# Token spans inside the weight loop: a new order for the products of the fill and the merge of an encoder layer

## The chip, the cores and the metric

The kernel runs on one core of a Trainium2 chip. The metric is the time of one execution on the device in microseconds (us). Lower is better.

## What is computed

The reference is one bidirectional encoder layer with two branches, run over two token groups (1024 prompt tokens and 256 sample tokens, 1280 in all, model width 1024). Cut to what matters here:

```python
h = rmsnorm(x, norm_mix) * (1 + sc1) + sh1
p = h @ w_in                                   # p_mla, p_rwkv, p_gate (2 x 1024 columns)
o_mla  = mla_branch(p_mla, ...) @ w_mla_o      # attention, 8 heads
o_rwkv = rwkv_branch(p_rwkv, ...) @ w_rwkv_o   # a scan over the tokens, both ways
gm, gr = split(sigmoid(p_gate), 2)
x = x + g1 * ((gm * o_mla + gr * o_rwkv) @ w_out)
h = rmsnorm(x, norm_ffn) * (1 + sc2) + sh2
u, z = split(h @ w_ffn_in, 2)
x = x + g2 * ((silu(u) * z) @ w_ffn_out)
return rmsnorm(x, final_norm)
```

All of it is in float32. A matrix product is made of three matmuls on rounded halves (`hi` and `lo`): weights hi by tokens hi, weights hi by tokens lo, weights lo by tokens hi.

## The kernel before

Tokens lie along the free dimension, so that a tile of 128 output rows by n tokens is one accumulation in a bank of PSUM (128 x 512 float32). The stages follow one another: a first norm and the products of `w_in`, attention, then the scan of the rwkv branch, the merge of both branches, and the feed-forward layer with the final norm.

The scan (`phase_rwkv`) works in ten batches of 128 tokens, one after the other through a state `S`. Each batch is a long chain of small matmuls on TensorE, copies on ScalarE and VectorE, and an inversion of 16-wide blocks on VectorE. While it runs, `phase_fill` gives TensorE other work. That is 27 gate products (nine slices `j` of `w_in`, for token spans at 0 and 256, then 512 and 768, then 1024, each 256 wide), then two rounds of eight products with `w_mla_o`: one for tokens 0 to 511, and one for tokens 512 to 1023 together with 1024 to 1279. When it ends, `merge` does eight products with `w_rwkv_o` and eight with `w_out`, first for one span of 512 tokens (`early`, from 256), then for two spans (`late`: 512 tokens from 768, and 256 from 0).

The order of instructions on each engine is not written by hand. A planner works on the emitted program: each instruction has a priority, that of its place in the program or higher (scan steps are emitted with `high_priority`), and by the planner's own costs it puts the one of highest priority that could start into its engine's queue. Each engine then runs its queue in that order. The fill stands behind the scan in priority.

All products that the change touches go through `product` (line 1044). `weights` (line 1040) brings the weights of a product in blocks of 4 x 128 rows: SP loads `wraw`, ScalarE rounds it into `whi` (line 53), and GpSimd subtracts to get `wlo` (line 55). There are two buffers of each (`RB`, `WB` = 2). A product with `kt` = 8 (gates, `w_out`) has two such halves, and so holds both buffers; one with `kt` = 4 (`w_mla_o`, `w_rwkv_o`) has one. `parts` is a list of PSUM tiles, and each part a list of spans of tokens that share the tile side by side. The gates have one part of two spans of 256 (one span in the last nine), the late rounds have two parts of 512 and 256. The generator yields a part as soon as its matmuls are emitted, and the caller then emits what reads it: `gate` a tanh on ScalarE (line 1153), `mla_out` and `merge` a VectorE operation (lines 1189, 1115, 1128).

In `phase_fill` the PSUM pool `g.fp` has two buffers (`FP` = 2); in `merge` it is `g.mm`, with six. Two tile pairs hold the tokens of the gates, tags `x0` and `x1`; `load` (line 1141) fills each with four DMAs (line 1145) when the products that read it are done:

```python
for i, x in enumerate(xs):
    for j in js[len(both):]:
        gate(j, x)
    if s < 2 and i < len(spans[s + 1]):
        new.append(load(i, spans[s + 1][i]))
```

The second round of `mla_out` reads the slots of `x0` and `x1` again, and `mid`, the operand of the early merge, is allocated in the slot of `x1` after it. A row pool of four buffers (`FR` = 4) holds the `gt` and `xm` rows of `merge`: two spans take all four.

Of the kernel before, what the change touches and what calls it, by code (L numbers as in the profile page):

```python
# [6 lines left out]
F32 = mybir.dt.float32  # L7
# [7 lines left out]
P = 128  # L15
# [31 lines left out]
def split_w(g, src, kt, eng=None, tag="w", pool=None, width=P, rbufs=2, bufs=2):  # L47
    nc = g.nc
    pool = pool or g.wst
    raw = pool.tile([P, kt, width], F32, tag=tag + "raw", name="wraw", bufs=rbufs)  # L50
    nc.sync.dma_start(out=raw if len(src.shape) == 3 else raw.rearrange("p (d f) n -> p d f n", d=src.shape[1]), in_=src)
    hi = pool.tile([P, kt, width], F32R, tag=tag + "hi", name="whi", bufs=bufs)
    nc.scalar.copy(hi, raw)  # L53
    lo = pool.tile([P, kt, width], F32R, tag=tag + "lo", name="wlo", bufs=bufs)
    (eng or nc.gpsimd).tensor_tensor(lo, raw, hi, ALU.subtract)  # L55
    return hi, lo
# [983 lines left out]
def weights(g, src, kt):  # L1040
    return [split_w(g, src[:, k0:k0 + 4, :], 4, pool=g.fl, tag=g.ft, rbufs=RB, bufs=WB) for k0 in range(0, kt, 4)]


def product(g, src, kt, parts, ws=None):

    ws = ws or weights(g, src, kt)
    for part in parts:
        p = g.fp.tile([P, 512], F32, tag="mm", name="fp")
        c = 0
        for a, n in part:  # L1050
            for k in range(kt):
                wh, wl = ws[k // 4]
                for i, (ww, aa) in enumerate(((wh, a[0]), (wh, a[1]), (wl, a[0]))):
                    g.nc.tensor.matmul(p[:, c:c + n], lhsT=ww[:, k % 4, :], rhs=aa[:, k, :n],  # L1054
                                       start=(k == 0 and i == 0), stop=(k == kt - 1 and i == 2))
            c += n
        yield p[:, :c]


# [44 lines left out]
def merge(g, spans, ops, m, x1, row):  # L1104

    nc, io = g.nc, g.io
    cs = [slice(c0, c0 + n) for c0, n in spans]
    for dt in range(KT):
        ts = []
        for c, (c0, n) in zip(cs, spans):  # L1110
            ts.append((row("gt")[:, :n], row("xm")[:, :n]))
            for t, nm, k in zip(ts[-1], ("gate", "xm"), (8, 0)):
                nc.sync.dma_start(out=t, in_=g.scr[nm][k + dt, :, c])
        for p, c, (t, xm) in zip(product(g, io["w_rwkv_o"][dt], 4, [[x] for x in ops]), cs, ts):
            nc.vector.scalar_tensor_tensor(t, t, 1.0, p, ALU.add, ALU.mult)
            nc.gpsimd.tensor_tensor(t, t, xm, ALU.add)
            split_in(g, t, m[0][:, dt, c], m[1][:, dt, c])
    for dt in range(KT):
        xs = [row("xt")[:, :n] for _, n in spans]
        for c, x in zip(cs, xs):  # L1120
            nc.sync.dma_start(out=x, in_=io["xT"][dt, :, c])
        for p, x, (c0, n) in zip(product(g, io["w_out"][dt], KT, [[([y[:, :, c] for y in m], n)] for c, (_, n) in zip(cs, spans)]),
                                 xs, spans):
            for s, (s0, l) in enumerate(SEG):
                lo, hi = max(c0, s0), min(c0 + n, s0 + l)
                if lo < hi:
                    r = slice(lo - c0, hi - c0)
                    nc.vector.scalar_tensor_tensor(x1[:, dt, lo:hi], p[:, r], g.gh[:, dt, s:s + 1], x[:, r], ALU.mult, ALU.add)


def phase_fill(g):
# [17 lines left out]
    def gate(j, *parts, ws=None):  # L1149
        for p in product(g, io["w_in"][20 + j], KT, [[x[:2] for x in parts]], ws):  # L1150
            n, c0 = p.shape[-1], parts[0][2]
            t = row("gt", n)
            nc.scalar.activation(t, p, AF.Tanh, scale=0.5)
            nc.sync.dma_start(out=g.scr["gate"][j, :, c0:c0 + n], in_=t)
# [317 lines left out]
```

## Time and profile before

| | |
|---|---|
| median of 3 runs | 2723.12 us (2720.77 to 2726.25) |
| profiled execution | 2719.07 us |
| its span in the trace | 2717.4 us |
| mean granted TensorE clock | 0.957 |
| TensorE busy | 2547.4 us, 94% of the span |
| VectorE, ScalarE, GpSimd busy | 1326.4, 1020.0, 841.7 us |
| chain that ended last: matmuls of line 1054 (`product`) | 8% of the span |

The profile is of one execution; times in it are counted from the span's start. The fill begins at about 880 us and ends at about 1530 us, the merge ends at about 1742 us. A busy TensorE is not one at its peak, since matmuls are pipelined and their ends are modelled: the starts of successive matmuls tell the rate. 1.00 of the granted clock is 2.4 GHz, 0.50 is 1.2 GHz.

### The profile page before, as it was taken

Reading aid. Unit: us, or ns where it says so; the run is one execution under the profiler, and the core shown is the slowest. Engines: PE = TensorE matmul, PEld = TensorE weight load, DVE = VectorE, ACT = ScalarE, POOL = GpSimd, SP = SyncE. Lnnn points to the kernel's source line nnn. Section 1 sums busy time; section 2 is a strip of 40 time slices with the busy share of each in tenths; the row PEclk is TensorE's granted clock in tenths of the full one; section 3 lists DMA queues with packets and bytes.
Section 4 is the critical chain, followed back from the end, with each engine's and each line's share of the span. In section 5 each row is a group of like instructions: output and inputs, shape, how many; then the busy total and the mean of one; then the engine's idle time right before and its main releaser. Section 6 shows DMA issues by size and latency. Waiting matters only on the chain.

```text
span 2717.4 us, 47321 instructions
## 1 busy us (share of the span) xinstructions
PE 2547.4 (94%) x19578; PEld 2160.1 (79%) x19578; DVE 1326.4 (49%) x2138; ACT 1020.0 (38%) x1913; POOL 841.7 (31%) x824
## 2 busy tenths in 40 slices
PE   5999999989997899999998988999999999999997
PEld 3777778778886788988877767778888888888886
DVE  6665562367776374565646557462222222222228
ACT  4433333257676565565653233241110111101114
POOL 1112131011115455454634466342111111111123
PEclk8999999999998798998988989999999999999998
DMA  7655531110013334444445655221111110111113
GB/s 294 226 185 198 188 146 63 45 29 18 20 32 107 103 107 137 141 114 137 126 147 164 191 182 154 92 71 55 39 39 39 39 36 35 39 39 39 39 40 132
DMA packets 178120, 273.80 MB, mean 101 GB/s; under 512 B 15008, under 2 KB 104944, under 8 KB 177904
## 3 DMA queue, kind: packets, MB, share of 16 engines
q1 hardware_dynamic: 164512, 223.19, 25.8%
q0 software_dynamic: 5760, 26.22, 2.4%
q10 hardware_dynamic: 7632, 21.37, 2.3%
q8 instruction: 154, 2.52, 0.4%
q14 instruction: 62, 0.51, 0.1%
HBM read 202.52 MB, written 68.20 MB: 100 GB/s over the span
## 4 chain that ended last, share of the span: by engine, by line
PE 75%; DVE 11%; ACT 5%; DMA 4%; issue 3%; POOL 2%; SPq 0%; DVEq 0%; POOLq 0%; ACTq 0%
PE mm L67 42%; PE fp L1054 8%; PE s L626 3%; PE o L660 2%; PE gps L453 2%; PE pA L819 2%; PE proj L559 2%; PE t L647 2%; PE py L927 2%; DMA ld<-scr_s 1%; PE pS L939 1%; PE py L945 1%; PE lora L369 1%; PE ada_ps L170 1%; PE py L933 1%
## 5 line engine op out<-in xcount | busy, mean ns | idle before, releaser
L55 POOL TENSOR_TENSOR wlo<-wraw,whi 128x512 fp32r<-128x512 f32 (+3 forms) x233 | 406.5, 1748 | 1177.6 <-ACT whi L53 1166.7
L53 ACT CAST whi<-wraw 128x512 fp32r<-128x512 f32 (+2 forms) x248 | 194.5, 789 | 898.0 <-issue 466.7
L67 PE MATMUL mm<-h2h,whi 128*128 128x512 f32 (+1 forms) x1056 | 279.2, 358 | 2.9 <-ACT whi L53 2.9
L67 PE MATMUL mm<-h2h,wlo 128*128 128x512 f32 (+1 forms) x1056 | 278.4, 357 | 1.1 <-POOL wlo L55 1.1
L67 PE MATMUL mm<-h2l,whi 128*128 128x512 f32 (+1 forms) x1056 | 278.2, 357 | 0.0
L67 PE MATMUL mm<-g,whi 128*128 128x512 f32 (+1 forms) x1056 | 240.6, 359 | 6.2 <-DVE ft L1259 5.6
L1054 PE MATMUL fp<-x,whi 128*128 128x256 f32 (+1 forms) x912 | 211.1, 324 | 11.7 <-ACT x L1036 5.0
L67 PEld LDWEIGHTS mm<-g,whi 128*128 128x128 f32 x1056 | 177.8, 190 | 38.0 <-issue 5.7
L67 PEld LDWEIGHTS mm<-h2h,whi 128*128 128x128 f32 x1056 | 177.1, 189 | 34.6 <-ACT whi L53 3.4
L67 PEld LDWEIGHTS mm<-h2h,wlo 128*128 128x128 f32 x1056 | 176.8, 188 | 32.7 <-POOL wlo L55 2.0
L67 PEld LDWEIGHTS mm<-h2l,whi 128*128 128x128 f32 x1056 | 176.9, 188 | 31.2 <-issue 0.5
L1271 DVE SCALAR_TENSOR_TENSOR x<-mm,g2h,x 128x512 f32<-128x512 f32 (+1 forms) x144 | 87.0, 655 | 196.3 <-PE mm L67 196.0
L1054 PEld LDWEIGHTS fp<-x,whi 128*128 128x128 f32 x912 | 157.6, 206 | 23.9 <-ACT x L1036 6.1
L67 PE MATMUL mm<-hl,whi 128*128 128x512 f32 (+1 forms) x480 | 147.5, 364 | 7.7 <-DVE hl L265 7.7
L67 PE MATMUL mm<-hh,whi 128*128 128x512 f32 (+1 forms) x480 | 148.1, 366 | 6.4 <-ACT pp L320 3.8
L1054 PE MATMUL fp<-x,wlo 128*128 128x256 f32 (+1 forms) x456 | 147.8, 325 | 6.3 <-POOL wlo L55 6.3
L1259 DVE SCALAR_TENSOR_TENSOR ft<-ft,mm 128x512 f32<-128x512 f32 (+1 forms) x66 | 36.0, 594 | 225.6 <-ACT ft L1258 225.6
L67 PE MATMUL mm<-hh,wlo 128*128 128x512 f32 (+1 forms) x480 | 145.8, 363 | 0.0
L1260 DVE TENSOR_TENSOR ft<-ft,mm 128x512 f32<-128x512 f32 (+1 forms) x66 | 36.0, 593 | 217.5 <-PE mm L67 217.5
L67 PE MATMUL mm<-g,wlo 128*128 128x512 f32 (+1 forms) x528 | 136.2, 359 | 1.4 <-POOL wlo L55 1.4
L626 PE MATMUL s<-kb,q 128*128 128x512 f32 (+1 forms) x432 | 112.0, 392 | 2.3 <-ACT pr L632 2.2
L67 PEld LDWEIGHTS mm<-hh,whi 128*128 128x128 f32 x480 | 84.5, 191 | 27.8 <-issue 6.9
(331 smaller groups left out, 5239.2 us busy)
## 6 DMA issues: line engine op xcount, KB each, us to landing
wraw<-in_w_ffn_in_dram SPq DMA_DIRECT2D x56, 512.0 KB, 3.5
wraw<-in_w_in_dram SPq DMA_DIRECT2D x68, 256.0 KB, 3.6
araw<-in_w_ada_dram ACTq DMA_DIRECT2D x32, 512.0 KB, 3.6
wraw<-in_w_ffn_out_dram SPq DMA_DIRECT2D x26, 512.0 KB, 3.6
wraw<-in_w_in_dram SPq DMA_DIRECT2D x20, 512.0 KB, 3.8
x<-scr_h SPq DMA_DIRECT2D x20, 512.0 KB, 7.5
araw<-in_w_ada_dram SPq DMA_DIRECT2D x16, 512.0 KB, 9.3
gt<-scr_gate SPq DMA_DIRECT2D x32, 256.0 KB, 2.7
```

What stands on the lines that cost most here:

```text
L53: nc.scalar.copy(hi, raw)
L55: (eng or nc.gpsimd).tensor_tensor(lo, raw, hi, ALU.subtract)
L67: nc.tensor.matmul(p[:, :n], lhsT=ww[:, k, :], rhs=aa[:, k, c0:c0 + n], start=(k == 0 and i == 0), stop=(k == kt - 1 and i == 2))
L453: nc.tensor.matmul(p[:, :n], lhsT=ww[:, k % 4, :], rhs=aa[:, k, c0:c0 + n], start=(k == 0 and i == 0), stop=(k == KT - 1 and i == 2))
L559: nc.tensor.matmul(p[:, :n], lhsT=ww[:, k, :], rhs=aa[:, k, c0:c0 + n], start=(k == 0 and i == 0), stop=(k == kt - 1 and i == 2))
L626: nc.tensor.matmul(s[:, o:o + w], lhsT=a[:, tt * P:(tt + 1) * P], rhs=b[:, c0 + o:c0 + o + w], start=(m == 0), stop=(m == 2))
L647: nc.tensor.transpose(t[:, j, :], prs[i][:, kk * P:(kk + 1) * P], g.ident)
L660: nc.tensor.matmul(o, lhsT=vs[h // 4][:, c0 // P + kk, h % 4, :], rhs=pts[j][m][kk // 4][:, kk % 4, :], start=(kk == 0 and m == 0), stop=( ...
L819: nc.tensor.matmul(pA[e][:, pt], lhsT=bk[HV[e], 2 * pt + sl], rhs=lt[HV[e], pt, e], start=True, stop=True)
L927: nc.tensor.matmul(py[e][HV[r], c, :], lhsT=lt[:, HV[r]], rhs=xv[:, u, e, :], start=(u == 0), stop=(r == 0 and u == 7))
L1054: g.nc.tensor.matmul(p[:, c:c + n], lhsT=ww[:, k % 4, :], rhs=aa[:, k, :n], start=(k == 0 and i == 0), stop=(k == kt - 1 and i == 2))
L1271: nc.vector.scalar_tensor_tensor(x1[:, dt, c0:c0 + n], p[:, :n], g.g2h[:, dt, c0 // TP:c0 // TP + 1], x1[:, dt, c0:c0 + n], ALU.mult, ALU.add)
```

## The change

`product` now emits its matmuls with the spans in the innermost loop. For each block of 128 rows of weights, and for each of the three combinations of halves, all spans of all parts come one after another. All PSUM tiles of the product are taken at its beginning, and all parts are yielded at its end. In a tile that two spans share, only the first span's first matmul has `start`, and only the last span's last has `stop`. Products with a single span come out in the same order as before: those are the last nine gates, the first round of `mla_out`, and the early merge.

```diff
     ws = ws or weights(g, src, kt)
-    for part in parts:
-        p = g.fp.tile([P, 512], F32, tag="mm", name="fp")
+    ps = [g.fp.tile([P, 512], F32, tag="mm", name="fp") for _ in parts]
+    todo, ends = [], []
+    for p, part in zip(ps, parts):
         c = 0
-        for a, n in part:
-            for k in range(kt):
-                wh, wl = ws[k // 4]
-                for i, (ww, aa) in enumerate(((wh, a[0]), (wh, a[1]), (wl, a[0]))):
-                    g.nc.tensor.matmul(p[:, c:c + n], lhsT=ww[:, k % 4, :], rhs=aa[:, k, :n],
-                                       start=(k == 0 and i == 0), stop=(k == kt - 1 and i == 2))
+        for j, (a, n) in enumerate(part):
+            todo.append((p[:, c:c + n], a, n, j == 0, j == len(part) - 1))
             c += n
+        ends.append(c)
+    for k in range(kt):
+        wh, wl = ws[k // 4]
+        for i, (ww, e) in enumerate(((wh, 0), (wh, 1), (wl, 0))):
+            for p, a, n, first, last in todo:
+                g.nc.tensor.matmul(p, lhsT=ww[:, k % 4, :], rhs=a[e][:, k, :n], start=(k == 0 and i == 0 and first),
+                                   stop=(k == kt - 1 and i == 2 and last))
+    for p, c in zip(ps, ends):
         yield p[:, :c]
```

## Rows read from the trace of the kernel before

**Rows 1.** Busy time of the engines in stretches of the scan and fill, in us, with the number of instructions in brackets: PE, PEld, DVE, ACT, POOL, then the granted clock, the DMA share and GB/s.
```profile
880.00:950.00 70.00, 59.63 (x674) 52.22 (x675) 24.69 (x55) 35.86 (x83) 33.31 (x52) 0.70 0.39 116
...
1478.00:1530.00 52.00, 52.00 (x600) 45.92 (x595) 15.50 (x26) 14.99 (x26) 11.53 (x9) 1.00 0.50 152
```

**Rows 2.** The timeline (start us, duration us): ScalarE's copy of a batch's output (line 948, the second of each batch) for the two neighbouring batches furthest apart of the ten, and for the two closest, which are the last; then the four splits that make `mid`.
```profile
1232.11 0.58 ACT L948 COPY yt<-py 64x512 f32<-64x512 f32 x1 [5.80 <-PE py L945]
1296.36 0.58 ACT L948 COPY yt<-py 64x512 f32<-64x512 f32 x1 [4.32 <-PE py L945]
...
1475.30 0.58 ACT L948 COPY yt<-py 64x512 f32<-64x512 f32 x1 [3.09 <-PE py L945]
1527.96 0.58 ACT L948 COPY yt<-py 64x512 f32<-64x512 f32 x1 [3.27 <-PE py L945]
1530.80 2.17 ACT L1036 CAST or<-wg 128x512 fp32r<-128x512 f32 x4
```

**Rows 3.** Who waited for whom, the five longest in total of TensorE's matmuls, 875 to 1362 us: us in total, times, longest.
```profile
PE pS L939 <- ACT xv L934: 6.3, 5, 1.8
PE pz L878 <- DVE xr L869: 4.7, 1, 4.7
PE py L933 <- DVE ru L931: 4.0, 3, 2.7
PE fp L1054 <- POOL wlo L55: 3.9, 2, 3.0
PE py L933 <- ACT tt L898: 3.1, 3, 1.2
```

**Rows 4.** The timeline of a gate product's end: the next product's two roundings of weights; then the paired subtractions of both halves, first and last of five such pairs from 1019 to 1261 us.
```profile
1065.20 0.62 ACT L53 CAST whi<-wraw 128x512 fp32r<-128x512 f32 x1
1071.12 0.62 ACT L53 CAST whi<-wraw 128x512 fp32r<-128x512 f32 x1
...
1019.95 2.49 POOL L55 TENSOR_TENSOR wlo<-wraw,whi 128x512 fp32r<-128x512 f32 x2 [0.19 <-POOL arb L737]
...
1260.70 2.50 POOL L55 TENSOR_TENSOR wlo<-wraw,whi 128x512 fp32r<-128x512 f32 x2 [0.19 <-POOL arb L737]
```

**Rows 5.** The timeline of the loads of `x` (SP's queue: start of the first, time to the issue of the last, count), how long such a load takes from issue to landing, and fill matmuls around them: first and last of the 15 of the first product before 890 us, first and last of the 13 after the first reload, and the last before and the first after the second reload.
```profile
1076.41 7.26 SPq L1145 DMA_DIRECT2D x<-scr_h  x8
...
1252.34 2.02 SPq L1145 DMA_DIRECT2D x<-scr_h  x4
...
x<-scr_h SPq DMA_DIRECT2D x8, 512.0 KB, 7.2
...
885.52 0.56 PE L1054 MATMUL fp<-x,wlo 128*128 128x256 f32 x1
889.87 0.40 PE L1054 MATMUL fp<-x,whi 128*128 128x256 f32 x2
...
1083.88 0.50 PE L1054 MATMUL fp<-x,whi 128*128 128x256 f32 x2
1085.41 0.28 PE L1054 MATMUL fp<-x,whi 128*128 128x256 f32 x1
...
1256.33 0.28 PE L1054 MATMUL fp<-x,wlo 128*128 128x256 f32 x1
1261.42 0.79 PE L1054 MATMUL fp<-x,whi 128*128 128x256 f32 x2
```

**Rows 6.** The timeline of the second round of `mla_out`: the first matmuls of a product's 512-wide part, VectorE's read of the 256-wide part of the product before, and its read of the 512-wide part.
```profile
1478.45 0.63 PE L1054 MATMUL fp<-x,whi 128*128 128x512 f32 x2
...
1478.65 0.42 DVE L1189 SCALAR_TENSOR_TENSOR gt<-gt,fp 128x256 f32<-128x256 f32 x1
1481.41 0.69 DVE L1189 SCALAR_TENSOR_TENSOR gt<-gt,fp 128x512 f32<-128x512 f32 x1 [1.71 <-PE fp L1054]
```

**Rows 7.** The timeline of `w_out` for two spans: successive matmuls of 512 and of 256 columns; and, in the feed-forward layer, successive groups of three matmuls of 512, 512 and 256 columns on the same weights.
```profile
1682.81 0.39 PE L1054 MATMUL fp<-h2h,whi 128*128 128x512 f32 x1
1683.05 0.39 PE L1054 MATMUL fp<-h2l,whi 128*128 128x512 f32 x1
...
1685.04 0.28 PE L1054 MATMUL fp<-h2h,whi 128*128 128x256 f32 x1
1685.16 0.28 PE L1054 MATMUL fp<-h2l,whi 128*128 128x256 f32 x1
...
2000.25 0.74 PE L67 MATMUL mm<-h2h,wlo 128*128 128x512 f32 x3
2000.83 0.75 PE L67 MATMUL mm<-h2h,whi 128*128 128x512 f32 x3
```

**Rows 8.** VectorE's reads of the 512-wide parts of `w_rwkv_o` for two spans: first and last of eight.
```profile
1630.15 0.69 DVE L1115 SCALAR_TENSOR_TENSOR gt<-gt,fp 128x512 f32<-128x512 f32 x1 [0.65 <-PE fp L1054]
...
1682.11 0.67 DVE L1115 SCALAR_TENSOR_TENSOR gt<-gt,fp 128x512 f32<-128x512 f32 x1
```

**Rows 9.** In the chain of waits, VectorE's last read of `w_out` (start us, us), and the engines' busy time behind it, in the columns of rows 1.
```profile
1742.32 0.48 DVE x L1128
...
1746.00:1752.00 6.00, 2.01 (x3) 0.99 (x4) 5.14 (x4) 1.04 (x1) 4.66 (x2) 0.50 0.30 97
1752.00:1756.00 4.00, 4.00 (x10) 2.64 (x9) 2.07 (x4) 0.59 (x1) 0.00 (x0) 0.53 0.31 117
1756.00:1760.00 4.00, 4.00 (x19) 3.22 (x18) 4.00 (x9) 1.94 (x4) 1.91 (x2) 1.00 0.00 0
```

## The prediction, written before the changed kernel was run

> **What bounds the kernel now.** I read the busy time by stretches first, then the timeline where the fill ends, then the waits of TensorE. In the stretches of scan and fill TensorE is the fullest engine: 59.63 of 70 us where it starts, 52.00 of 52 in the second round of `mla_out` [rows 1]. The scan goes at about 60 us a batch whatever the fill gives it, between 64.3 (1232.11 to 1296.36) and 52.7 us (1475.30 to 1527.96, the last) [rows 2]. The scan's last copy is at 1527.96, and the four splits that make `mid` follow in one piece from 1530.80. `mid` lies in the slot of `x1`, so these splits wait for the last fill product. Scan and fill therefore end together, and the end of the fill starts the early merge. A microsecond that TensorE loses before 1530 can be lost for good, unless the planner puts scan work into it.
>
> The waits then say what the change can win. Of the five longest waits of TensorE up to 1362 us, four are scan steps that wait for ScalarE or VectorE (6.3 + 4.7 + 4.0 + 3.1 = 18.1 us). The fill's wait for `wlo` is 3.9 us, in two events [rows 3]. After the first products the weights hardly hold up TensorE any more.
>
> **What the change does to the weights.** In a gate product of two spans the first half of the weights serves matmuls 1 to 12 and 25 to 36 of 48. The trace shows it: the next product's first rounding starts at 1065.20, its second at 1071.12 [rows 4], with the product's last 12 matmuls and scan work between them. Afterwards the first half is free after 24, and the next product needs its second half only at its 25th matmul, not at its 13th. The lead grows from 12 matmuls to 24. At 0.12 us for 256 columns (1685.04 to 1685.16 [rows 7]) it grows from 1.4 to 2.9 us. A rounding of 0.62 and a subtraction of about 1.25 us (half a pair [rows 4]) are 1.9 us: 12 matmuls don't cover it alone, 24 do. So the two events may go: -3.9 us, bounds 0 and -3.9. I take all of it.
>
> The two subtractions that stand as a pair of 2.5 us at a product's end, five times [rows 4], come apart as well, which lets the scan's GpSimd work pass sooner. Bounds are 0 and -5 x 1.25 = -6.3; I take -2, since a pair only counts where the scan's chain waits behind it.
>
> **What each matmul costs.** It stays the same. Successive matmuls are 0.24 us apart at 512 columns and 0.12 at 256. The feed-forward layer has the order that `product` gets now, 512, 512 and 256 on the same weights, and its groups of three are 0.58 us apart, where the single ones sum to 0.60 [rows 7]. Nothing is saved or lost by alternating. The late `w_out`, whose matmuls already come without a gap, gains nothing.
>
> **What comes later: the tokens.** Both spans are now needed from the first two matmuls, and both are in use until the last. There are three places.
> - At the start, eight loads go through SP one after the other. The eight of the first reload took 7.26 us to issue [rows 5], so the second pair stands up to 3.6 us behind the first. In the kernel before, 15 matmuls run on the first span between 885.52 and 889.87 [rows 5]. That is cover that goes: 15 x 0.12 = 1.8 us at full clock, twice that at half. Bounds 0 and +3.6; I take +2.
> - At the change to the second spans, the loads of `x0` start at 1076.41, in mid-product, and the fill resumes at 1083.88. The last of the eight is issued at 1076.41 + 7.26 = 1083.67, and with 7.2 us to landing it is there at 1090.9 [rows 5]. Moved to the product's end, `x0` no longer runs ahead, but the end of the issues hardly moves, and the scan's loads behind them on SP's queue neither. The fill then has to wait for `x1`. What it did meanwhile is 13 matmuls, 1.6 us; the wait is 7.0 us if no scan work takes its place. I take +1.6, since the scan has work there; bounds 0 and +7.0.
> - At the change to the last span, the four loads start at 1252.34, and the product's last matmul is at 1256.33 [rows 5]. They start 4 us later, so bounds are 0 and +4.2. I take +0.5: the row at 1261.42 holds only two fill matmuls.
>
> **What comes later: the parts.** In the second round of `mla_out` the 512-wide part of a product starts at 1478.45, before VectorE has read the 256-wide part of the product before (1478.65), because its own buffer was read in the middle of that product [rows 6]. Now both buffers fill up together, and the next product waits for reads of 0.69 and 0.42 us [rows 6]. Seven boundaries give 0 to 7 x 1.11 = +7.8 us. The stretch has no idle time to give, but it has scan pieces that can move into the gap. I take a quarter, +2.
>
> In the late `w_rwkv_o` eight reads of the 512-wide part go from 1630.15 to 1682.11, 7.4 us a product [rows 8], while its matmuls need 12 x (0.24 + 0.12) = 4.3 us. The rows and what follows the products set this pace, and the weights have no part in it. Only its beginning moves: the first 512-wide part ends 12 x 0.12 = 1.4 us later. I take +1.4, bounds 0 and +1.4.
>
> Behind the last `w_out` product only one read of 0.48 us stands before the next norm [rows 9]. Now the 512-wide read stands there too, in two pieces across the groups: +0.69 to +1.1 by the reads in [rows 6]. I take +1.1, lower bound 0.
>
> **The sum.** -3.9 - 2 + 2 + 1.6 + 0.5 + 2 + 1.4 + 1.1 = +2.7 us. On the profiled execution that is 2719.07 + 2.7 = 2721.8. That execution lies 4.05 us below the median of 2723.12, so the forecast is 2725.8. All favourable bounds together give -10.2 (2712.9), all unfavourable ones +25.1 (2748.2). A difference of 0.2%, 5.4 us, is about what a measurement of this kernel can tell from none. On top of the sum, the planner writes a new order for the whole scan. Batches that do the same work already differ by 11.6 us [rows 2].
>
> **Rivals.**
> - *Starved by the tokens (slower).* The three token waits stay open: 3.6 + 7.0 + 4.2 = 14.8 us. After such gaps the clock is low: behind a gap of about 4 us the granted clock reads 0.50, then 0.53 over the next 4 us of matmuls, then 1.00 [rows 9]. That is some 2 us for each of the two larger gaps. With the other terms, except those of `mla_out`, at -3.9 - 2 + 1.4 + 1.1, it is +15.4, so 2738.5. For it: rows 5 show the first reload arriving just as the fill resumes. Against it: high-priority scan work that can fill the gap. It decides once more than about 9 of the 14.8 us are uncovered. The Trainium skill (TensorE: Matmul & The Clock Gate, "HAM oscillation — how this bites in real kernels") says that idle gaps bring the clock back to its low level; by this rule the trace agrees, with 0.50 behind the gap in rows 9.
> - *Held by PSUM (slower).* The seven boundaries of `mla_out` cost their full 7.8 us: 2725.8 + 5.8 = 2731.6. For it: VectorE is in order and shares its queue with the scan. Against it: the scan pieces.
> - *Better packed (faster).* With weights always ahead, the planner can put fill into the 18.1 us in which TensorE waits in scan steps [rows 3]. Half of that and the 3.9 give -13, so 2710.1. Against it: only 3.9 us of the waits name the weights.
> - *It does nothing:* the planner had the weights covered by scan work, and the new order is as good: 2723.1. It lies in the forecast's case.
>
> **Chances and range.** No change within 0.2%: 0.37 (2717.7 to 2728.6, with the forecast and the last rival). Starved by the tokens 0.22 and held by PSUM or a worse order 0.13: slower 0.35. Better packed: faster 0.28. The range for 8 in 10 reaches into both, from 2708 to 2742.
>
> **What would show it.** If right: the fill's `wlo` waits before 1362 us are gone; the roundings of weights lie evenly, not in pairs; the `x` loads start at the products' ends with a hole in the fill of some 5 us behind them; the late `w_out` takes the same time; the merge begins within 5 us of 1531. The forecast is wrong if the scan's batches change their pace by more than 1 us each, or if the gaps at the reloads are idle.

## The result: slower by 0.66%, and the profile after

The changed kernel takes 2741.09 us (median of 11 runs, 2730.28 to 2748.62); the kernel before, run beside it, takes 2723.12 us (11 runs, 2707.78 to 2734.18). The ratio is 1.0066 with a 95% interval of 1.0041 to 1.0091. That is +18 us. The profiled execution took 2733.93 us, its span is 2732.2 us and its mean granted clock 0.950. All lines of `kernel.py` behind `product` are six higher: line 1054 is now 1060, 1145 is 1151, 1153 is 1159, 1189 is 1195, 1115 is 1121, 1128 is 1134.

First the place. These are ScalarE's second copies of a batch's output (line 948) after batches 2, 3, 4 and 10, and the splits that make `mid`:

```profile
1048.60 0.58 ACT L948 COPY yt<-py 64x512 f32<-64x512 f32 x1 [1.29 <-PE py L945]
1124.93 0.58 ACT L948 COPY yt<-py 64x512 f32<-64x512 f32 x1 [4.48 <-PE py L945]
1196.03 0.58 ACT L948 COPY yt<-py 64x512 f32<-64x512 f32 x1 [7.22 <-PE py L945]
...
1540.85 0.58 ACT L948 COPY yt<-py 64x512 f32<-64x512 f32 x1 [0.76 <-PE py L945]
1550.60 2.17 ACT L1036 CAST or<-wg 128x512 fp32r<-128x512 f32 x4
```

Batches 3 and 4 take 76.3 and 71.1 us. The kernel before has the same copies here:

```profile
1053.91 0.58 ACT L948 COPY yt<-py 64x512 f32<-64x512 f32 x1 [2.37 <-PE py L945]
...
1173.44 0.58 ACT L948 COPY yt<-py 64x512 f32<-64x512 f32 x1 [3.52 <-PE py L945]
```

So 147.4 us stand against 119.5, which is +27.9, while after batch 2 the changed kernel was 5.3 us ahead. Of these 22.6 us the scan wins 9.7 back by its end (1540.85 against 1527.96 [rows 2], +12.9). The fill now ends later still: the splits of `mid` start at 1550.60, 19.8 us behind [rows 2]. The last read of `w_out` is at 1760.47 to 1761.74; before, it ended at 1742.80 [rows 9], so the changed kernel is 18.9 us behind there. The spans of these two executions differ by 14.8 us, so 4.1 of the 18.9 are won back behind the merge; the medians of all runs differ by 18.

The busy time by stretches says of what kind the loss is. The first fence is the kernel before, batches 3 and 4, the second the changed one (columns as in rows 1, clock behind the brackets):

```profile
1053.90:1111.90 58.00, 57.27 (x922) 53.30 (x923) 30.95 (x69) 33.62 (x74) 29.29 (x39) 0.86 0.58 174
1111.90:1173.40 61.50, 59.35 (x962) 54.35 (x960) 37.04 (x71) 37.53 (x83) 30.55 (x41) 0.97 0.37 105
```

```profile
1048.60:1124.90 76.30, 69.26 (x953) 62.47 (x954) 33.39 (x70) 35.00 (x76) 28.76 (x40) 0.75 0.46 139
1124.90:1196.00 71.10, 69.68 (x977) 64.31 (x978) 32.14 (x70) 38.49 (x84) 32.22 (x43) 0.87 0.30 91
```

TensorE's idle time grows from 119.5 - 116.62 = 2.9 to 147.4 - 138.94 = 8.5 us, only +5.6. The clock is lower as well: span times (1 - clock), which is what the clock falls short of full speed, is 58.0 x 0.14 + 61.5 x 0.03 = 10.0 us before and 76.3 x 0.25 + 71.1 x 0.13 = 28.3 us after, +18.3. Idle time at a low clock counts in both sums. The count of matmuls is nearly the same (1884 and 1930).

Not all of this lies behind the reload of `x`, the fill's change from its first pair of token spans to the second. Here are the same stretches cut at 1081 us, where the fill's first round ends in the changed kernel; the kernel before comes first:

```profile
1053.90:1081.00 27.10, 27.10 (x497) 25.09 (x497) 14.10 (x40) 13.17 (x28) 7.65 (x12) 0.77 0.29 91
1081.00:1173.40 92.40, 89.52 (x1385) 82.56 (x1385) 53.89 (x100) 57.98 (x129) 52.19 (x67) 0.96 0.52 152
```

```profile
1048.60:1081.00 32.40, 31.83 (x445) 28.19 (x447) 12.61 (x39) 9.07 (x18) 4.58 (x6) 0.64 0.16 50
1081.00:1196.00 115.00, 107.11 (x1485) 98.59 (x1485) 52.92 (x101) 64.41 (x143) 56.41 (x76) 0.85 0.45 134
```

Up to 1081 span times (1 - clock) is 27.1 x 0.23 = 6.2 us before and 32.4 x 0.36 = 11.7 us after. So some 5 of the 18 us are lost ahead of the reload. Both kernels have a clock of 0.50 at the start of batch 3, behind waits of TensorE at the end of batch 2 (2.69 us at 1049.25 before; 1.44 at 1047.36 and 0.57 at 1049.88 after), and it stays low for longer in the changed one.

Now the chain of waits through the first reload. After:

```profile
1075.51 5.52 PE fp L1060 x32
1081.17 6.07 DMA x<-scr_h
...
1106.53 1.28 POOL bk L788
...
1107.95 4.50 DMA ld<-scr_s
1112.48 1.23 DVE L L773
...
1117.94 0.61 DVE ru L931
```

And before:

```profile
1073.98 1.13 PE pw L896 x64
1075.12 4.26 PE fp L1054 x34
...
1086.91 10.32 DMA ld<-scr_s
1097.25 1.24 DVE L L773
```

Before, the scan's 64 small matmuls (line 896) stand ahead of the round's last 34 fill matmuls. These run while ScalarE copies for the scan, and no load of `x` is on the chain (a load of the scan is, with 10.32 us). After, the fill's last matmuls stand ahead of the scan's 64, and nothing is left behind them. The load of `x` is on the chain with 6.07 us. In the timeline the 64 matmuls start 20.0 us after the end of batch 2 before (1053.91 to 1073.91) and 32.4 us after it in the changed kernel (1048.60 to 1080.95). So 12.4 of the 27.9 us are there before these matmuls start, and 15.5 come behind. TensorE shows the same:

```profile
1080.95 1.20 PE L896 MATMUL pw<-dt,aa 32*32 32x32 f32 x64
1084.51 1.16 PE L819 MATMUL pA<-lt,bk 64*128 64x128 f32 x8 [2.36 <-ACT arb L828]
1087.28 0.58 PE L1060 MATMUL fp<-x,whi 128*128 128x256 f32 x1 [0.77 <-DMA x<-scr_h]
1094.65 0.63 PE L1060 MATMUL fp<-x,whi 128*128 128x256 f32 x3
...
1118.60 1.96 PE L933 MATMUL py<-ru,tt 64*64 64x64 f32 x16 [3.34 <-DVE ru L931]
```

After 1081 only one fill matmul runs before 1094.65, a hole of 13.7 us; before it was 1079.4 to 1083.88, 4.5 us [rows 5]. On SP's queue the scan's loads go out late as well:

```profile
1080.70 1.48 SPq L1151 DMA_DIRECT2D x<-scr_h  x3
1082.78 7.28 SPq L1151 DMA_DIRECT2D x<-scr_h  x5
1094.00 0.37 SPq L754 DMA_DIRECT2D ld<-scr_s  x1
1107.95 0.50 SPq L754 DMA_DIRECT2D ld<-scr_s  x1
```

The last load of `x` is issued at 1082.78 + 7.28 = 1090.06, not at 1083.67 [rows 5]. The scan's own loads behind it go out at 1094.00 and 1107.95; before, these were at 1086.91 and 1102.26, so they are 7.1 and 5.7 us later. But the trace doesn't show the loads of `x` holding them. The last issue ahead of them ends at 1090.16 + 1.30 = 1091.46, and then SP waits for VectorE:

```profile
SPq L754 <- DVE lt L806: 1.9, 1, 1.9
```

The second one follows GpSimd's line 788 on the chain above. Lines 806 and 788 are steps of the scan, and the scan's 64 matmuls themselves start 7.0 us later (1080.95, not 1073.91). So the late loads show that the scan is late; they are not shown to make it so. VectorE then waits for the second (line 773 at 1112.48), and the copy `ru` stands behind that in its queue until 1117.86. Hence the gap of 3.34 us on TensorE at 1118.60. The new plan has a part in this gap: in the kernel before, `ru` stands ahead of the second line 773 in VectorE's queue:

```profile
1102.09 0.68 DVE L931 COPY ru<-py 64x512 f32<-64x512 f32 x1
...
1105.84 1.23 DVE L773 TENSOR_TENSOR_SCAN L<-rst,ld 128x512 f32<-128x512 bf16 x1 [0.29 <-DMA ld<-scr_s]
```

The clock around the gap in the changed kernel, in steps of 5 us:

```profile
1110.00:1115.00 5.00, 5.00 (x118) 4.67 (x119) 3.60 (x4) 3.27 (x8) 4.15 (x7) 1.00 0.15 43
1115.00:1120.00 5.00, 1.66 (x41) 1.56 (x32) 3.53 (x9) 2.87 (x8) 2.60 (x3) 0.66 0.65 195
1120.00:1125.00 5.00, 5.00 (x70) 4.61 (x68) 1.52 (x3) 0.52 (x2) 1.64 (x2) 0.50 0.41 123
1125.00:1130.00 5.00, 5.00 (x64) 4.43 (x61) 1.38 (x2) 1.09 (x2) 1.20 (x3) 0.50 0.02 3
1130.00:1135.00 5.00, 5.00 (x34) 4.25 (x35) 0.00 (x0) 2.97 (x7) 0.00 (x0) 0.50 0.23 52
1135.00:1140.00 5.00, 5.00 (x151) 4.72 (x151) 0.14 (x1) 0.00 (x0) 0.11 (x1) 0.79 0.01 3
```

From 1.00 the clock falls to 0.66 in the stretch of the gap and to 0.50 behind it, which is 1.2 GHz, and stays there for three rows although TensorE is busy for 5.00 of 5.00 us in each: with scan matmuls of 16 to 128 columns, and no fill until 1133.26. The Trainium skill (TensorE: Matmul & The Clock Gate, "HAM oscillation — how this bites in real kernels") says that a wait of TensorE lowers its clock, and its example pays about 1.67 us at the low clock for each wait. The trace agrees that a gap brings the clock down; the time at the low level is some 15 us here, and the measurement decides.

### The profile page after: what moved, and what is told of

It is laid out like the page before. It is cut to its first block, busy times and chain, and to the rows that moved or that the text cites. A ratio compares the mean times of both kernels' runs of the same rounds, so it can differ in the third digit from the quotient of the medians.

```text
span 2732.2 us, 47307 instructions
## 1 busy us (share of the span) xinstructions
PE 2559.2 (94%) x19578; PEld 2171.5 (79%) x19578; DVE 1321.8 (48%) x2138; ACT 1022.5 (37%) x1913; POOL 840.2 (31%) x824
## 4 chain that ended last, share of the span: by engine, by line
PE 75%; DVE 13%; DMA 4%; ACT 4%; issue 2%; POOL 2%; SPq 1%; DVEq 0%; POOLq 0%; ACTq 0%
PE mm L67 42%; PE fp L1060 8%; PE s L626 3%; PE o L660 2%; PE gps L453 2%; PE pA L819 2%; PE proj L559 2%; PE t L647 2%; PE py L927 2%; DMA ld<-scr_s 1%; PE py L945 1%; PE pS L939 1%; PE py L933 1%; PE ada_ps L170 1%; PE lora L369 1%
## 5 line engine op out<-in xcount | busy, mean ns | idle before, releaser
L1060 PE MATMUL fp<-x,whi 128*128 128x256 f32 (+1 forms) x912 | 198.5, 327 | 8.0 <-DMA x<-scr_h 3.3
L1060 PEld LDWEIGHTS fp<-x,whi 128*128 128x128 f32 x912 | 150.1, 210 | 18.9 <-issue 3.8
L1060 PE MATMUL fp<-x,wlo 128*128 128x256 f32 (+1 forms) x456 | 121.0, 323 | 3.7 <-POOL wlo L55 3.7
```

The costliest lines, as they stand in the source:

```text
L1060: g.nc.tensor.matmul(p, lhsT=ww[:, k % 4, :], rhs=a[e][:, k, :n], start=(k == 0 and i == 0 and first), stop=(k == kt - 1 and i == 2 and last))
```

## Experiments

All but e5, e6, e11 and e12 choose between two orders for each product. The order of the kernel after is called *inside* (spans in the inner loop), that of before *outside*. A kernel with both has this instead of `product`:

```python
def product(g, src, kt, parts, ws=None):
    return (spans_inside if inside else spans_outside)(g, src, kt, parts, ws)
```

and only the condition `inside` differs; the conditions below are shortened. Each ratio is to the kernel before on the same chip (medians 2722.72, 2722.64 and 2721.34 us for the three groups e1 to e4, e5 to e8, e9 to e12).

### e1 and e2: which products

```diff
+    inside = len(parts) == 1       # e1: the gates
+    inside = len(parts) > 1        # e2: second round of mla_out, late merge
```

> Spans inside only where they share one PSUM tile (the 18 gate products of two spans); the second round of mla_out and the late merge in the old order. Measured for the whole change: +18 us at the median (ratio 1.0066). Theory 1 (the tokens of the next spans come late, and on SP's queue the scan's loads come late behind them): the scan's last copy stays about 10 us later than before and the kernel is +10 to +18 us. Theory 2 (the pair of PSUM tiles in mla_out and merge): 0 to +5 us. Theory 3 (any newly planned order of the scan gives this much, no part carries it): anywhere from -10 to +20 us.

> Spans inside only where a product has two PSUM tiles (second round of mla_out, late merge); the gates in the old order. Theory 1: 0 to +6 us, the reloads of x start at about 1076 us as before. Theory 2: +10 to +18 us, with idle time at the product boundaries of mla_out. Theory 3: -10 to +20 us.

Measured: e1 2745.56 us, ratio 1.0073 (1.0046 to 1.0101); e2 2723.94 us, 1.0007 (0.9985 to 1.0029). As far as these intervals tell, the loss sits in the 18 gate products of two spans. The terms of the sum for `mla_out` and the merge come to nothing that can be measured.

### e3 and e4: the last product of a round

In e3 the last gate product before each reload is outside and all else as in the change; in e4 these two products alone are inside.

```diff
+    inside = not g.last            # e3
+    inside = g.last                # e4
+        g.last = j == 15 and len(parts) > 1
```

> The whole change, but the last gate product before each of the two reloads of x has its spans outside, as before, so that x0 is free in the middle of it. Theory 1: most of the loss goes, 0 to +8 us against before; the first reload starts before its product ends and the fill hole behind it is about 5 us, not 14. Theory 2: stays at +14 to +20 us. Theory 3: -10 to +20 us.

> The kernel before, but the last gate product before each of the two reloads of x has its spans inside, so that x0 and x1 are free only at its end: two of 43 products are changed. Theory 1: +6 to +18 us, with the first reload starting at the product's end and a fill hole of more than 8 us behind it. Theory 2: within 3 us of before. Theory 3: -10 to +20 us.

Measured: e3 2726.59 us, 1.0008 (0.9988 to 1.0028); e4 2726.90 us, 1.0016 (0.9996 to 1.0037). With the last two products undone the loss is gone. But they alone bring little of it, less than the +6 to +18 us that theory 1 asked for. So it takes their order and the others' together. The trace of e3 shows what its last product changes. The loads of `x` start at 1074.95, in mid-product, and the chain goes from the fill's last matmuls to the scan, with no load of `x` on it:

```profile
1072.55 5.51 PE fp L1076 x32
1078.06 1.16 PE pw L896 x64
...
1090.74 3.60 DMA ld<-scr_s
```

All but four of the fill's last matmuls stand ahead of the scan's 64, much as in the changed kernel, and batch 3 is long too (70.0 us), but batch 4 takes 58.7.

### e5 and e6: the plan and the weights

e5 only exchanges two combinations of halves in the kernel before, to see what a new plan alone may do. e6 has all products of several spans in the order: first half of the weights for each span, then second half for each. Its weights come free after 24 and 48 matmuls, as in the change.

```diff
-                for i, (ww, aa) in enumerate(((wh, a[0]), (wh, a[1]), (wl, a[0]))):
+                for i, (ww, aa) in enumerate(((wh, a[1]), (wh, a[0]), (wl, a[0]))):
```

```diff
-    for k in range(kt):
-        wh, wl = ws[k // 4]
-        for i, (ww, e) in enumerate(((wh, 0), (wh, 1), (wl, 0))):
-            for p, a, n, first, last in todo:
+    for k0 in range(0, kt, 4):
+        wh, wl = ws[k0 // 4]
+        for p, a, n, first, last in todo:
+            for k in range(k0, k0 + 4):
+                for i, (ww, e) in enumerate(((wh, 0), (wh, 1), (wl, 0))):
```

> The kernel before with the first two combinations of halves exchanged in product (weights hi by tokens lo first, then weights hi by tokens hi): same matmuls, same weights, same spans, another order to plan. Theory 1 (tokens at the reloads): within 4 us of before. Theory 3 (any new plan moves the time by so much): as far from before as the changed kernel, 8 us or more to either side. It sizes the noise of planning for the other runs.

> The change one step coarser: the first half of the weights for the first span, then for the second, then the second half for each. The weights are freed as in the changed kernel (after 24 and 48 matmuls), x0 is freed after 36 of 48 and x1 is needed from the 13th matmul. Theory 1: most of the loss gone, 0 to +8 us. If the weights' release were the cause: +12 to +20 us, as the changed kernel. Theory 3: -10 to +20 us.

Measured: e5 2728.78 us, 1.0031 (1.0006 to 1.0055); e6 2722.01 us, 0.9995 (0.9971 to 1.0019). So a new plan can cost 0.3% by itself, which is half of the loss in question: the 8 us of theory 3, not the 4 of theory 1. And the earlier release of the first half of the weights brings neither a gain nor a loss that can be measured.

### e7 and e8: the products around the reload

In e7 the whole change is made, but the first product behind the first reload is outside, so that it can start with one span's tokens. In e8, the last product of both rounds and the first of the second round are inside, all else outside.

```diff
+    inside = not g.edge            # e7
+    inside = g.edge                # e8
+        g.edge = len(parts) > 1 and (j == NB and parts[0][2] == 512)               # e7
+        g.edge = len(parts) > 1 and (j == 15 or j == NB and parts[0][2] == 512)    # e8
```

> The whole change, but the first gate product on the reloaded spans has its spans outside, so that it can run 24 matmuls on x0 before it needs x1; x0 and x1 are still freed only at the end of the product before. Theory 1, hole at the resumption: 0 to +8 us, the fill resumes with more than 10 matmuls. If the late issue of the loads alone counts (the scan's loads behind them on SP): +12 to +20 us, as the changed kernel. Theory 3: -10 to +20 us.

> The kernel before, but three gate products have their spans inside: the last before each reload and the first after the first reload. So x0 is free late and x1 is needed at once, at the one place. Theory 1: +10 to +20 us, batches three and four of the scan longer by 10 us or more together. Theory 3 or another cause in the other gate products: within 5 us of before.

Measured: e7 2740.07 us, 1.0073 (1.0050 to 1.0096); e8 2723.02 us, 1.0008 (0.9987 to 1.0029). In e7 the fill resumes with 13 matmuls on one span, and the loss stays: that the next product needs both spans at once is not the cause. In the trace of e8 the fill has one matmul between 1081.5 and 1100.4 us, a hole longer than that of the changed kernel, and the runs show no loss, where theory 1 asked for +10 to +20 us. So a hole alone isn't the cause either. (The profiled execution of e8 is a long one, 2734.86 us.)

### e9 and e10: which round

```diff
+    inside = g.edge
+        g.edge = len(parts) > 1 and (parts[0][2] == 0)      # e9: first round (tokens at 0 and 256)
+        g.edge = len(parts) > 1 and (parts[0][2] == 512)    # e10: second round
```

> The spans stand inside the weights' loop only in the nine gate products of the first round (tokens at 0 and 256); the second round's nine gates, mla_out and the merge are as before. Theory 'the end of the first round': the loss of batches 3 and 4 belongs to the first round's own order and its late last product, so the ratio is 1.005 to 1.009 and batches 3 and 4 take over 140 us together. Rival 'the second round': what holds the scan is the resumed products of the second round, which need both spans at once, and the ratio is within 0.2% of 1. Rival 'chance of the plan': any change of the plan near the reload can fall on either side, and then the ratio says nothing about the round; it would show in a ratio of about 1.003.

> The spans stand inside the weights' loop only in the nine gate products of the second round (tokens at 512 and 768). Theory 'the end of the first round': within 0.2% of the kernel before, with batches 3 and 4 at 118 to 128 us together. Rival 'the second round': 1.005 to 1.009. If both this kernel and the one with the first round alone are within 0.2%, the loss needs both rounds, that is a late end of the first round and products behind it that need both spans at once.

Measured: e9 2733.28 us, 1.0055 (1.0034 to 1.0075); e10 2728.24 us, 1.0025 (1.0003 to 1.0047). The first round seems to bring more of the loss, though the two intervals overlap. In e9 batches 3 and 4 take 75.6 and 66.1 us; e10 has 55.0 and 62.7. What e10 loses is within what e5 shows for a new plan; in its trace a load of `x` is on the chain at the second reload, with 6.93 us (from 1260.10). The chain of e9 at the reload is that of the changed kernel:

```profile
1077.56 5.22 PE fp L1060 x32
...
1082.91 6.30 DMA x<-scr_h
...
1089.25 3.15 PE fp L1076 x13
```

### e11 and e12: the queue of the loads

The loads of `x` are issued from GpSimd's queue, in the changed kernel (e11) and in the kernel before (e12).

```diff
-                nc.sync.dma_start(out=a[e][:, k:k + KS].bitcast(F32),
+                nc.gpsimd.dma_start(out=a[e][:, k:k + KS].bitcast(F32),
```

> The whole change, with the loads of x issued from GpSimd's queue, not from SP's. If the loss comes from SP's queue (the loads of x stand behind a load of weights and ahead of the scan's loads, which then arrive late), the scan's loads are no longer behind the x loads, and the ratio falls to within 0.25% of 1. If it comes from the tokens themselves being asked for late, whatever queue they go through, or from the order of the matmuls, it stays at 1.005 to 1.009. GpSimd's own issue time stands before its scan work, which may cost some us in both.

> The kernel before, with the loads of x issued from GpSimd's queue, not from SP's: the control of the run before. Expected within 0.25% of the kernel before; if it is slower than that, the queue itself has a price, which is taken from the other kernel's ratio before that is read.

Measured: e11 2750.65 us, 1.0109 (1.0074 to 1.0144); e12 2735.79 us, 1.0052 (1.0024 to 1.0080). The other queue has a price of 0.5%, and the difference between the two is still 0.57%. But the plan turned round with it: now e11 has the scan's 64 matmuls ahead of the fill's last 34 (1074.23, then 1075.36), and e12 has the fill ahead (1078.10, then 1083.61). And in e11 a load of the scan stands on the chain with 12.11 us (line 754, from 1085.68). So this pair says that SP's queue alone isn't the cause. It also says that the order of these matmuls isn't needed for a loss of this size: e11 has it against its control without that order.

### What the experiments say together

| kernel | fill's last matmuls ahead of the scan's 64 | load of `x` on the chain | batches 3 + 4, us | ratio |
|---|---|---|---|---|
| before | no | no | 119.5 | 1 |
| after | yes | 6.07 us | 147.4 | 1.0066 |
| e1 | yes | not shown | 145.7 | 1.0073 |
| e7 | yes | 6.45 us | 139.5 | 1.0073 |
| e9 | yes | 6.30 us | 141.8 | 1.0055 |
| e3 | all but four | no | 128.7 | 1.0008 |
| e6 | all but six | not shown | 118.8 | 0.9995 |
| e4 | no | not shown | 123.7 | 1.0016 |
| e8 | no | no | 129.4 | 1.0008 |
| e10 | no | no | 117.7 | 1.0025 |

(The chain of e1 doesn't reach this stretch; its TensorE has the same waits there, 2.36 us for `arb` and 1.06 for `x`. The chains of e4 and e6 don't reach it either; TensorE's waits for `x` are 0.31 and 1.30 us there.) The column of batches is from one profiled execution each, the ratio from all runs. The profiled executions of e8 and e10 took 2734.86 and 2735.30 us, 12 and 7 us above their medians, and their scans end 14 and 25 us later than before's, with the time lost in other batches. So a low number in that column doesn't say that an execution loses nothing.

The four kernels of the table that lose 0.5% or more have two things at once at the end of the first round: the fill's last matmuls stand ahead of the scan's step, and the tokens are released only at the product's end. With either alone the loss isn't there (e3; e4 and e8). So theory 1 as first written, the late tokens alone, fails. That both parts are needed is suggested, not shown: each kernel is one plan, a plan alone can move 0.3% (e5), and e11 loses without the order. That the order of these few matmuls is the link between them is read from the traces; no run changed that order alone. A version that splits each tile of tokens in two, so that the order by k would release half of them early, was not tried on the chip.

The runs also tell, beyond one profile, how the loss divides by clock. Mean span and mean granted clock over all runs of a kernel, and span x (1 - clock) and span x clock, averaged over the runs:

```
            runs   span     clock    span x (1 - clock)   span x clock
before       29    2720.2   0.9551        122.2              2597.9
after        11    2739.1   0.9468        145.7              2593.4
e1            6    2743.6   0.9458        148.6              2595.0
e6           12    2721.0   0.9538        125.6              2595.4
e9           12    2732.6   0.9485        140.7              2591.9
e3           12    2725.4   0.9497        137.2              2588.2
```

The last column moves by 0.25% at most for the first five. What the changed kernel loses is +23.5 us in the fourth column, with -4.5 in the fifth. (In its other two groups of runs the kernel before has 125.4 and 124.7 in the fourth, so it is +20 to +24.) Idle time at a low clock counts in the fourth as well, and e3 shows that the two can offset each other: it has +15.0 in the fourth and -9.7 in the fifth, and a ratio of 1.0008. So the loss goes along with a lower clock; this division doesn't show that the clock is its cause.

## Why the prediction was right and wrong

The time lies within the range (2708 to 2742, at its upper end), and near the rival "starved by the tokens" (2738.5). The likeliest case, no change, did not come, and the sum, +2.7 us, is 15 us below the measured +18. That the time lies within is owed to the width of the range. By the steps:

- **Bound.** That the merge begins with the fill's end held: it begins 19.8 us later and its last read ends 18.9 later. That scan and fill end together held less well: 9.8 us lie between the scan's last copy and the splits (1540.85 and 1550.60), where 2.8 did [rows 2].
- **Weights, -3.9: not won.** The fill's waits for `wlo` up to 1362 us, against [rows 3]:

```profile
PE py L933 <- DVE ru L931: 6.3, 4, 3.3
PE pz L878 <- DVE xr L869: 4.0, 1, 4.0
PE pA L819 <- ACT arb L828: 3.8, 2, 2.4
PE fp L1060 <- POOL wlo L55: 3.7, 1, 3.7
PE fp L1060 <- DMA x<-scr_h: 3.3, 2, 2.5
```

  The 3.7 us remain as one wait, at 900.50. Before, the two were at 897.80 (0.90) and 902.45 (2.97). All three fall early in the second product, which should have had the longer lead as well; why its weights are late there is not shown. The prediction took a sum over 875 to 1362 us without asking when its two events were. e6, with the same release of weights, has 0.9995.
- **Pairs of subtractions, -2: not seen.** Some came apart (three pairs, at 1016.56, 1178.53 and 1218.92, where five were [rows 4]). No step of the scan that gained by it was found.
- **Matmuls cost the same: right.** In the changed kernel successive triples of reads of `w_out` stand 8.33 us apart (1752.14 to 1760.47), and six of them take 49.92 us; six took 49.90 before.
- **Tokens at the start, +2: hidden.** The first fill matmul starts at 880.16 against 879.76, and the run of fill matmuls behind it at 887.36 against 885.52, so some 1.8 us later as foreseen; the first batch's copy still comes 4 us sooner (986.9 against 990.9).
- **First reload, +1.6, bounds 0 and +7.0: the step that failed.** The sentence was that "the end of the issues hardly moves, and the scan's loads behind them on SP's queue neither". It moved by 6.4 us (1083.67 to 1090.06), since the loads start 4.3 us later and the last five take 7.28 us to issue. The scan's loads moved by 7.1 and 5.7 us, though not because of the queue: they followed the scan's own steps. The step also took for granted that the scan has work while the fill waits. It had too little: its 64 matmuls stood behind the fill's last ones, and ScalarE's copies behind them, for which TensorE waited 2.36 us. It priced the fill's wait, which was 0.77 us, and not what the scan loses in the new plan, nor the clock: of the +27.9 us in batches 3 and 4, 18.3 go with the clock, some 13 of them behind 1081.
- **Second reload, +0.5: right in effect.** Batches 6 and 7 take 58.9 and 59.2 us against 64.2 and 56.8, and TensorE's waits for `x` (3.3 us in two) are those at 880.16 (2.51) and 1087.28 (0.77).
- **`mla_out`, +2, `w_rwkv_o` and the norm, +2.5: not told from nothing.** e2 holds all three, and its ratio is 1.0007, that is +1.9 us with an interval of -4.1 to +7.9. TensorE is busy for 56.00 of 56 us from 1494 to 1550, and VectorE reads both parts together:

```profile
1494.00:1550.00 56.00, 56.00 (x673) 49.43 (x671) 18.50 (x31) 15.55 (x26) 13.96 (x11) 1.00 0.50 154
...
1506.16 1.02 DVE L1195 SCALAR_TENSOR_TENSOR gt<-gt,fp 128x512 f32<-128x512 f32 x2 [3.01 <-PE fp L1060]
```

  So the reads of both parts stand as a pair of 1.02 us at a product's end, as foreseen, and scan pieces fill the gap. The eight 512-wide reads of the late `w_rwkv_o` go from 1648.57 to 1699.83, 51.26 us against 51.96 [rows 8].
- **The rivals.** "Starved by the tokens" named the place and the clock, but made its price from three open waits and 2 us of clock for each gap. That its 2738.5 us lie near the measured time is luck: TensorE's waits for `x` add up to 3.3 us, where 2.3 were before, not to 14.8 us more. Most of the loss lies around the first reload, in the scan's batches. For the low clock it used the 4 us behind the gap in [rows 9], where matmuls of 512 columns follow; here only scan matmuls follow, and it lasted some 15 us. Its point of decision, 9 of 14.8 us uncovered, was not what decided. "Held by PSUM" falls with e2. "Better packed" falls with e6.
- **What would show it.** Two of its signs fired: scan batches that change by more than 1 us (batches 3 and 4 by +18.3 and +9.6), and a merge that doesn't begin within 5 us of 1531.

Open is why the planner puts the scan's 64 matmuls behind the fill's last ones in this plan, and line 773 ahead of `ru` on VectorE, and how much of the 0.66% another plan of the same change would keep: e5 shows that 0.3% can come from a plan alone.

## To carry over

When an order is moved from the outer to the inner loop, ask what each operand's last use is, and what the other work on the engine has to do while the reload is on its way: here the fill's own wait for its tokens was small, and what the scan lost around it was not. When a load goes out late, ask what its queue waited for: here it was the scan itself, not the loads ahead. If work is filler, its end is a place of its own: look at what the main chain has as cover in the few microseconds when the filler has run out, and at what clock it runs then. And give a sum over waits a look at when they fall, before a saving is made of it.

## Not expected of the hardware

- Behind one gap of 3.34 us the granted clock read 0.50 for three rows of 5 us although TensorE counted as busy throughout, on scan matmuls of 16 to 128 columns; at 1133.26 fill matmuls began, and the row from 1135 reads 0.79. The kernel before shows the same: behind the wait of 2.69 us at 1049.25, the clock reads 0.50 from 1050 to 1060 and 0.69 from 1060 to 1070, with TensorE counted as busy throughout.
- The times of the same kernel go along with its clock: over 29 runs of the kernel before, span and mean granted clock have a correlation of -0.85, with spans of 2704 to 2738 us and clocks of 0.948 to 0.962.
- When the eight loads of `x` met loads of weights and of the scan, the DMA share was 1.04 and 1.10 at 357 and 351 GB/s from 1085 to 1095 us (the last two columns below), and the scan's load `ld` issued at 1094.00 took 6.3 us from issue to landing. In the kernel before, the one issued at 1086.91 was on the chain for 10.32 us.

```profile
1085.00:1090.00 5.00, 4.23 (x30) 3.37 (x30) 0.69 (x1) 4.73 (x12) 3.74 (x9) 0.59 1.04 357
1090.00:1095.00 5.00, 5.00 (x67) 4.87 (x66) 2.73 (x4) 0.62 (x2) 2.56 (x5) 0.73 1.10 351
```
